# Sliding-window attention under projections: all five queues in one written order, exponentials a round behind, q's rotation in pieces

## The chip, the core and the metric

The kernel runs on one core of one Trainium2 chip. The metric is the time on the device in microseconds (us); of three runs the median is 1564.43 us (1564.02 to 1564.64). The engines are named as in the profile: PE multiplies matrices, PEld loads PE's weights, DVE is the vector engine, ACT the scalar engine, POOL the third elementwise engine, and SP only issues DMAs. Each has a queue of its own.

## What is computed

One decoder layer on 1024 tokens of width 1024: a combined projection, retention and sliding-window attention side by side, a gated merge, and a SwiGLU block. The part that the change touches is the attention, whose core is:

```python
scores = jnp.einsum('bnqhgd,bnkhd->bnhgqk', qb, kb).astype(jnp.float32) * (d ** -0.5)
...
scores = jnp.where(mask[None, :, None, None], scores, -1e30)
sink = sinks.astype(jnp.float32).reshape(1, 1, Hkv, G, 1, 1)
m = jnp.maximum(jnp.max(scores, axis=-1, keepdims=True), sink)
e = jnp.exp(scores - m)
probs = e / (jnp.sum(e, axis=-1, keepdims=True) + jnp.exp(sink - m))
out = jnp.einsum('bnhgqk,bnkhd->bnqhgd', probs.astype(v.dtype), vb)
```

There are 16 query heads of width 64 on 2 key heads, 8 blocks of 128 queries, and each block sees its own 128 keys and the 128 before. Queries and keys are rotated first. Beside it the kernel computes ten of the sixteen 128-column slabs of the two gate projections, `tanh((h @ W + b) / 2)`.

## The kernel before, in words

Every matrix product is made of three: each fp32 operand is split into a high half in a shorter format (a cast on ACT) and a low half (a subtraction on DVE), and high x high, high x low and low x high are added up. `H` holds the normalised input in both halves, transposed.

**Units and rounds.** The 16 heads form four groups g of four heads. A unit u is one group and one block b of queries (u = 8 g + b, 32 units). The loop `for i in range(NU + 2)` makes 34 rounds. Round i transposes the probabilities of unit i - 2 (`u_transpose`, L562), multiplies the scores of unit i (`u_scores`, L530), takes some steps of the fill, and multiplies the values of unit i - 2 (`u_values`, L580). So PE has the fill's products between the transposes and the values that need their result.

**One unit.** Eight products on PE write the scores `s` (negated, for 256 keys; 128 where b is 0). ACT copies the newer half to `sc` (L546), DVE lays the older half over it by a predicated copy (L547) and takes the minimum `nm` with the sink (L549); for b = 0 a custom operation does both (L552). ACT makes four exponentials with their sums (L555), DVE the reciprocal (L558) and the product (L559). PE transposes to `pT` (L567); ACT casts the high half `p` (L569), DVE makes its low half (L570) and a masked copy `q` of both (L575). PE multiplies `p` and `q` with the values to `pv` (L586), ACT copies that to `xy` (L589), and POOL stores it. POOL also writes the sinks into `sc` (L537).

**The fill.** `Fill` runs through a list of products a step (three matmuls) at a time: `QuadQ(1)`, two gates, `QuadQ(2)`, two gates, `QuadQ(3)`, six gates. A `QuadQ` makes the queries of a group, four products of 8 steps (`quad_q`, L478: two token halves by two rotary halves z), a gate two (`gate`, L592). 20 of the 256 steps come ahead of the rounds and 28 behind them; before, the first 16 rounds take 7 steps each and the other 18 some 5.3. `prep` casts an item's weights from a raw slab that SP has loaded (L442 for q, L467 for gates); there are two such slabs, and a load waits until the low half (L452, L473) has read the one before.

**Rotation.** `quad_q` evicts two products to `a` and `b` (ACT, L488), DVE makes six operations with the tables (L497 to L502), ACT and DVE split the result (L503 to L506). The four tiles `a`, `s2`, `s1`, `b` are stored to `q_d` and read back to the layout that the scores want (`send_turned`, L514): four stores and four reads a half, all on SP. `a` and `b` rotate through three buffers, `s1` and `s2` have one each, so the next half must wait for these stores.

**What sets the order.** Each engine works through its queue in order. The order is made when the kernel is built: a scheduler places instructions by priority, and `in_order(...)` pins the written order on the queues that it names. Before, it names PE and SP for the rounds; ACT, DVE and POOL are placed by the scheduler, with chains (`tie`) for the casts and low halves alone. Behind the rounds, DVE's first tiles of the next stage (`vacc`, L731) lie where the attention's tiles lay.

Of the kernel before, what the change touches and what calls it, by code (L numbers as in the profile page):

```python
# [40 lines left out]
def hybrid_block(ctx: ExitStack, tc: tile.TileContext, x, ln1_g, w_in, b_in, ret_norm_g, w_ret_out,  # L41
# [41 lines left out]
    def acc(name):  # L83
        return ps("acc", 3, name)
# [240 lines left out]
    with tc.tile_pool(name="gt", bufs=1, side="right") as gt, tc.tile_pool(name="w1", bufs=1) as w1:  # L325
        atab = w1.tile([P, 2, S], F32, name="atab")
# [6 lines left out]
        vodd = w1.tile([P, NB // 2, P], F32, tag="xy", bufs=2, name="vodd")  # L333
# [144 lines left out]
        def quad_q(g, w):  # L478
            if g % 2 == 0:
                big(B, "B", g // 2, f"q{g}")  # L480
            Bt = B[g // 2]
            jb = (g % 2) * 4
            ab = {}
            for half, z in ((0, 0), (0, 1), (1, 0), (1, 1)):
                pt = acc(f"aq{g}{z}{half}")
                yield from mm_g(pt, w[z], H, half * 512)
                t = r512("rab", 3, f"q{g}{z}{half}")
                nc.scalar.activation(t, pt, AF.Identity, bias=bcol[:, QB + 4 * z + g:QB + 4 * z + g + 1], scale=1.0)  # L488
                ab[z, half] = t
                if z == 0:  # L490
                    yield
                    continue
                c = slice(half * 512, half * 512 + 512)
                a, b = ab[0, half], t
                s1, s2 = (r512(f"st{i}", 1, f"st{i}{g}{half}") for i in (1, 2))
                cos, sin = atab[:, 0, c], atab[:, 1, c]
                nc.vector.tensor_tensor(out=s2, in0=a, in1=cos, op=ALU.mult)  # L497
                nc.vector.tensor_tensor(out=s1, in0=b, in1=sin, op=ALU.mult)
                nc.vector.tensor_tensor(out=s2, in0=s2, in1=s1, op=ALU.subtract)
                nc.vector.tensor_tensor(out=a, in0=a, in1=sin, op=ALU.mult)  # L500
                nc.vector.tensor_tensor(out=b, in0=b, in1=cos, op=ALU.mult)
                nc.vector.tensor_tensor(out=b, in0=b, in1=a, op=ALU.add)  # L502
                nc.scalar.activation(a.bitcast(F32R), s2, AF.Copy)  # L503
                nc.vector.tensor_tensor(out=s2.bitcast(F32R), in0=s2, in1=a, op=ALU.subtract)
                nc.scalar.activation(s1.bitcast(F32R), b, AF.Copy)
                nc.vector.tensor_tensor(out=b.bitcast(F32R), in0=b, in1=s1, op=ALU.subtract)  # L506
                turns.append((q_d[2 * g + half], (a, s1, s2, b), Bt[:, jb:jb + 4, c]))
                if g == 0 and half == 0:
                    send_turned()
                yield  # L510

        turns = []

        def send_turned():  # L514
            for qd, rows, o in turns:
                for r in (0, 2, 1, 3):
                    nc.sync.dma_start(qd[:, r, :], rows[r])
                for r in (0, 2, 1, 3):
                    nc.sync.dma_start(f32(o[r * 32:r * 32 + 32]), qd[:, r, :].rearrange("(j e) c -> e j c", e=32))
            turns.clear()  # L520
# [7 lines left out]
        phs = {}  # L528

        def u_scores(u):  # L530
# [3 lines left out]
            mk = amask[:, 0:P]  # L534
            sc = w1.tile([P, 4, 132], F32, tag="sc", bufs=3, name=f"sc{g}{b}")
            scs[u] = sc
            nc.gpsimd.tensor_copy(sc[:, :, P:P + 1], nsink[:, 4 * g:4 * g + 4].rearrange("p (j o) -> p j o", o=1))  # L537
            nm = tiny.tile([P, 4], F32, tag="nm", name=f"nm{g}{b}")
# [1529 lines left out]
```

## Time and profile before

| what | before |
|---|---|
| median of 3 runs | 1564.43 us |
| the profiled execution | 1560.39 us, its span 1558.6 us |
| mean granted clock of PE | 0.998 |
| PE busy | 1539.6 us, 99% |
| DVE, ACT, POOL busy | 1030.0, 690.5, 404.2 us |
| 78 to 190 us (rounds 0 to 14): PE, DVE, ACT busy of 112 us | 107.58, 81.94, 65.35 us |
| 190 to 305 us (the later rounds): the same of 115 us | 111.22, 87.52, 70.62 us |

The profile is one execution, taken by the hardware profiler; its times are from the span's start. "Idle before" an instruction is time in which its engine did nothing, with what ended that. The chain is the work that ended last, followed back from the last instruction. PE's matmuls overlap, so their durations add up to more than their time.

### The profile page before, as it was taken

How to read it: one execution, taken by the hardware profiler on the slowest of the kernel's cores; microseconds unless marked ns; L12 is line 12 of the kernel's file. 1: busy time of each engine (PE TensorE's matmuls, PEld its weight loads, DVE VectorE, ACT ScalarE, POOL GpSimd, SP SyncE). 2: the span in 40 equal slices, each digit the busy share in tenths (PEclk: the TensorE clock that was granted, in tenths of full speed). 3: DMA queues.
4: the chain of work that ended last, by engine and by line, in shares of the span. 5: the costliest groups of instructions: out<-in, count | busy, mean ns of one | idle time of the engine just before them, and what ended most of it. 6: DMA issues, size and time to landing. Idle time of an engine off the chain costs nothing.

```text
span 1558.6 us, 20393 instructions
## 1 busy us (share of the span) xinstructions
PE 1539.6 (99%) x7311; PEld 1283.1 (82%) x7311; DVE 1030.0 (66%) x1566; ACT 690.5 (44%) x1360; POOL 404.2 (26%) x356
## 2 busy tenths in 40 slices
PE   9999999999999999999999999999999999999998
PEld 8887787788878888888888888888888888888886
DVE  7577787697477683878557788444444444678656
ACT  6355565533334454544223365333333333444445
POOL 2001111100254431000021124655555555100001
PEclk9999999999999999999999999999999999999999
DMA  6663546321777766654555303333333333863233
GB/s 229 194 189 117 162 152 232 134 69 68 202 199 223 216 203 212 228 178 152 181 182 205 146 1 107 105 107 107 108 102 102 101 102 102 305 242 95 89 108 121
DMA packets 159025, 236.86 MB, mean 152 GB/s; under 512 B 10602, under 2 KB 82092, under 8 KB 158668
## 3 DMA queue, kind: packets, MB, share of 16 engines
q1 hardware_dynamic: 156316, 227.04, 45.2%
q0 software_dynamic: 2560, 8.39, 1.4%
q8 instruction: 57, 0.93, 0.3%
q14 instruction: 44, 0.36, 0.1%
q10 hardware_dynamic: 48, 0.13, 0.0%
HBM read 156.62 MB, written 74.19 MB: 148 GB/s over the span
## 4 chain that ended last, share of the span: by engine, by line
PE 88%; DVE 4%; DMA 3%; ACT 2%; issue 1%; SPq 1%; POOL 0%; POOLq 0%; DVEq 0%; ACTq 0%
PE fA L1692 15%; PE fB L1692 8%; PE dA L1994 7%; PE wA L957 7%; PE dxP L1994 6%; PE fC L1692 4%; PE wB L957 3%; PE va L800 3%; PE wo L1526 3%; PE woP L1526 2%; PE vP L800 2%; PE acc_ba L178 2%; PE acc_ba L180 2%; PE acc_ba L179 2%; PE acc_bb L179 2%; PE acc_bb L180 2%
## 5 line engine op out<-in xcount | busy, mean ns | idle before, releaser
L1994 PE MATMUL dA<-dwP,daP 128*128 128x512 f32 x528 | 120.6, 389 | 0.0
L1994 PEld LDWEIGHTS dA<-dwP,daP 128*128 128x128 f32 x528 | 99.1, 188 | 20.7 <-DVE dwP L154 0.2
L1994 PE MATMUL dxP<-dwP,daP 128*128 128x512 f32 x396 | 90.2, 389 | 0.0
L1994 PEld LDWEIGHTS dxP<-dwP,daP 128*128 128x128 f32 x396 | 74.3, 188 | 15.4
L555 ACT ACTIVATE sc<-sc,nm 128x129 f32<-128x129 f32 x128 | 50.1, 394 | 44.3 <-DVE nm L549 32.0
L1767 POOL TENSOR_TENSOR xf<-xf 128x512 f32<-128x512 f32 x40 | 59.9, 1497 | 30.5 <-issue 28.9
L178 PE MATMUL acc_g<-h,wh_g 128*128 128x512 f32 x160 | 62.7, 392 | 0.0
L1698 POOL TENSOR_TENSOR xf<-xf 128x512 f32<-128x512 f32 x33 | 47.3, 1435 | 58.7 <-ACT xf L1700 26.9
L179 PE MATMUL acc_g<-h,wh_g 128*128 128x512 f32 x160 | 62.5, 391 | 0.0
L180 PE MATMUL acc_g<-h,wl_g 128*128 128x512 f32 x160 | 62.3, 389 | 0.0
L537 POOL COPY sc<-nsink 128x4 f32<-128x4 f32 x32 | 10.1, 317 | 189.5 <-PE pT L567 83.1
L1899 POOL TENSOR_TENSOR rs_f<-tot,mhalf 128x1 f32<-128x1 f32 x8 | 4.8, 604 | 205.4 <-DVE tot L1896 205.4
L154 DVE TENSOR_TENSOR dwP<-wd,dwP 128x512 fp32r<-128x512 f32 x77 | 52.8, 686 | 4.8 <-ACT dwP L151 4.8
L151 ACT CAST dwP<-wd 128x512 fp32r<-128x512 f32 x77 | 47.4, 616 | 9.1 <-PE dA L1994 6.9
L178 PE MATMUL acc_bb<-ay,wh_bb 128*128 128x512 f32 x128 | 51.0, 400 | 0.0
L669 POOL TENSOR_TENSOR wr_f<-wr_f 128x512 f32<-128x512 f32 x20 | 30.7, 1533 | 76.0 <-DVE t_18P L154 8.6
L180 PE MATMUL acc_bb<-ay,wl_bb 128*128 128x512 f32 x128 | 50.3, 393 | 0.0
L151 ACT CAST daP<-daP 128x512 fp32r<-128x512 f32 x42 | 26.0, 621 | 54.8 <-PE dxP L1994 26.7
L179 PE MATMUL acc_bb<-ay,wh_bb 128*128 128x512 f32 x128 | 50.2, 392 | 0.0
L178 PE MATMUL aq<-h,wh_aq 128*128 128x512 f32 x128 | 50.1, 392 | 0.0
L179 PE MATMUL aq<-h,wh_aq 128*128 128x512 f32 x128 | 50.0, 391 | 0.0
L178 PE MATMUL acc_ba<-yg,wh_ba 128*128 128x512 f32 x128 | 49.9, 390 | 0.0
(852 smaller groups left out, 4305.2 us busy)
## 6 DMA issues: line engine op xcount, KB each, us to landing
act_d<-xf SPq DMA_DIRECT2D x77, 256.0 KB, 2.1
daP<-act_d SPq DMA_DIRECT2D x21, 512.0 KB, 3.6
q<-q_d SPq DMA_DIRECT2D x32, 256.0 KB, 5.0
xy_d<-xy POOLq DMA_DIRECT2D x32, 256.0 KB, 3.0
wr_daP<-act_d SPq DMA_DIRECT2D x14, 512.0 KB, 6.7
wd<-in_w_ffn_down SPq DMA_DIRECT2D x6, 1024.0 KB
wr_wp<-in_w_in SPq DMA_DIRECT2D x11, 512.0 KB, 3.7
wp<-in_w_in SPq DMA_DIRECT2D x11, 512.0 KB
```

What stands on the lines that cost most here:

```text
L151: nc.scalar.copy(hi, raw)
L154: return nc.vector.tensor_tensor(out=lo, in0=raw, in1=f32(hi), op=ALU.subtract)
L178: nc.tensor.matmul(pt, hi[:, k, :], xh, start=(k == 0), stop=False)
L179: nc.tensor.matmul(pt, hi[:, k, :], xl, start=False, stop=False)
L180: nc.tensor.matmul(pt, lo[:, k, :], xh, start=False, stop=(k == 7))
L555: nc.scalar.activation(sc[:, j, 0:P + 1], sc[:, j, 0:P + 1], AF.Exp, scale=-1.0, bias=nm[:, j:j + 1], accum_out=den[:, j:j + 1])
L800: nc.tensor.matmul(vbanks[pr][tt], x_[:, c], w[:, u, :], start=(fresh and k + z == 0), stop=(k == 3 and z == 2), skip_group_check=not fresh)
L957: nc.tensor.matmul(pt, o[:, w, k, :], v, start=(first and k + z == 0), stop=(k == 3 and z == 2), skip_group_check=not first)
L1526: nc.tensor.matmul(bank, v[:, q + u, k, c], w[y][:, k % 2, :], start=(first and z == 0), stop=(last and z == 2), skip_group_check=not tracked)
L1692: nc.tensor.matmul(pt, o[:, w, k, :], v, start=(first and n == 0), stop=(n == 11), skip_group_check=not first)
L1767: nc.gpsimd.tensor_tensor(out=o, in0=a, in1=b, op=op)
L1994: nc.tensor.matmul(banks[tt], a[:, u, c], w[:, v, :], start=(fresh and f + z == 0), stop=(f == NP - 1 and z == 2), skip_group_check=not fresh)
```

## The change

**One written order.** `in_order` now names all five queues for the rounds. What stood inside `u_scores` becomes four functions: `u_sink` (POOL, a round ahead), `u_scores` (PE alone), `u_min` (copy, predicated copy, minimum) and `u_exp` (exponentials, reciprocal, product), and `u_exp` handles unit i - 1 in round i.

**q by token halves.** `quad_q` goes half by half. Its rotation is cut into three tasks (three products, three products, the split with its stores), and a round takes one task off a list: its ACT part behind `u_min`, its DVE and SP parts behind the fill steps. The eviction of the last product of a group waits in the list too, joined to the first task of its half. A half's read-back is issued in the round after its stores, behind `u_min`. For group 0 all tasks run at once.

**Pacing and the rest.** The first 21 rounds take 140 steps, the other 13 take 68. The four 1 MB loads of `wv` are issued in rounds 20, 22, 24 and 26 instead of all in round 20. `vodd` is the first tile of its pool instead of the seventh. The core of the diff:

```diff
+            for half in range(2):
+                c = slice(half * 512, half * 512 + 512)
+                ab = []
+                for z in range(2):
+                    pt = acc(f"aq{g}{z}{half}")
+                    yield from mm_g(pt, w[z], H, half * 512)
...
+                    if z and half:
+                        tasks.append(([evict], [], []))
+                    else:
+                        evict()
+                    if z:
+                        rotation(g, half, c, ab, Bt[:, jb:jb + 4, c])
+                        if g == 0:
+                            all_tasks()
                     yield
...
+            first = [start, lambda: tt(s2, a, cs, ALU.mult), lambda: tt(s1, b, sn, ALU.mult),
+                     lambda: tt(s2, s2, s1, ALU.subtract)]
+            if tasks and not tasks[-1][1]:
+                tasks[-1][1].extend(first)
+            else:
+                tasks.append(([], first, []))
+            tasks.append(([], [lambda: tt(a, a, sn, ALU.mult), lambda: tt(b, b, cs, ALU.mult),
+                               lambda: tt(b, b, a, ALU.add)], []))
+            tasks.append(([lambda: high(a, s2), lambda: high(s1, b)],
+                          [lambda: low(s2, s2, a), lambda: low(b, b, s1)], [store]))
...
-        early, late = 16 * 7, 96
-        with in_order(nc.tensor.engine, nc.sync.engine):
+        early, late, turn = 140, 68, 21
+        with in_order(nc.tensor.engine, nc.sync.engine, nc.scalar.engine, nc.vector.engine, nc.gpsimd.engine):
+            u_sink(0)
             for i in range(NU + 2):
...
                 if i < NU:
                     u_scores(i)
-                n, i0, m = (early, 0, 16) if i < 16 else (late, 16, NU - 14)
+                if 0 < i <= NU:
+                    u_exp(i - 1)
+                if i < NU:
+                    u_min(i)
+                while reads:
+                    reads.pop(0)()
+                on_act, on_dve, on_sp = task()
+                do(on_act)
+                if i + 1 < NU:
+                    u_sink(i + 1)
+                n, i0, m = (early, 0, turn) if i < turn else (late, turn, NU + 2 - turn)
                 fl.step((i - i0 + 1) * n // m - (i - i0) * n // m)
+                do(on_dve)
+                do(on_sp)
                 if i > 1:
                     u_values(i - 2)
```

Lines of the new kernel that the text names: L492 the eviction, L514 the rotation's products, L530 and L533 the split, L521 and L526 the stores and reads, L581 scores, L590 to L593 copy to minimum, L596 the same for b = 0, L604 exponentials, L607 and L608 reciprocal and product, L616 transposes, L618, L619 and L624 `p`, its low half and `q`, L635 values, L638 the copy to `xy`, L716 the loads of `wv`.

What this does to ACT's queue shows in a round of the second group. Names carry a buffer number; `pT` is read by the cast to `p`, `wh_aq` are high halves of q's weights. Before:

```order
L589 COPY xy_1903<-pv_1898 128x512
L546 COPY sc_1916<-s_1920 128x4x128
L555 ACTIVATE sc_1916,den_1919<-sc_1916,nm_1918 128x129 x4
L451 CAST wh_aq_1889<-wr_aq_1698 128x512
L569 CAST p_1911<-pT_1906 128x512
L597 ACTIVATE tb_1945<-acc_g_0_1873,bhalf 128x512
L589 COPY xy_1969<-pv_1964 128x512
```

After, the same kind of round:

```order
L618 CAST p_1875<-pT_1870 128x512
L604 ACTIVATE sc_1762,den_1764<-sc_1762,nm_1763 128x129 x4
L590 COPY sc_1830<-s_1880 128x4x128
L530 ACTIVATE q_1617<-st_1789 128x512
L530 ACTIVATE st_1788<-q_1760 128x512
L451 CAST wh_aq_1917<-wr_aq_1623 128x512
L451 CAST wh_aq_1917<-wr_aq_1702 128x512
L646 ACTIVATE tb_1932<-acc_g_0_1855,bhalf 128x512
L638 COPY xy_1946<-pv_1941 128x512
```

The cast to `p` moved from behind the exponentials and the weight cast to the head of its round, and the exponentials now read minima of the round before.

SP's queue ahead of the first rounds: `wr_g` are raw slabs of gates, `wr_aq` of q, `q_d` the stores of a turned half, `q_675<-q_d` its read-back. Before:

```order
L519 DMA q_675<-q_d 32x4x512 x4
L467 DMA wr_g_832<-in_w_in 128x8x128
L467 DMA wr_g_834<-in_w_in 128x8x128
L517 DMA q_d<-q_775 128x512
L517 DMA q_d<-st_811 128x512
L517 DMA q_d<-st_810 128x512
L517 DMA q_d<-q_808 128x512
L519 DMA q_675<-q_d 32x4x512 x4
L442 DMA wr_aq_965<-in_w_in 128x4x256
```

After:

```order
L526 DMA q_675<-q_d 32x4x512 x4
L521 DMA q_d<-q_775 128x512
L521 DMA q_d<-st_811 128x512
L521 DMA q_d<-st_810 128x512
L521 DMA q_d<-q_808 128x512
L526 DMA q_675<-q_d 32x4x512 x4
L467 DMA wr_g_840<-in_w_in 128x8x128
L467 DMA wr_g_842<-in_w_in 128x8x128
L442 DMA wr_aq_950<-in_w_in 128x4x256
L442 DMA wr_aq_1013<-in_w_in 128x4x256
```

The loads of the first two gates moved behind the stores and the read-back of the second half of group 0, and the second of group 2's loads moved up: before, it stood behind the read-back of both halves of group 1 (eleven rows further on).

SP's queue where the last group is turned, before:

```order
L467 DMA wr_g_2285<-in_w_in 128x8x128
L517 DMA q_d<-q_2094 128x512
L517 DMA q_d<-st_2204 128x512
L517 DMA q_d<-st_2203 128x512
L517 DMA q_d<-q_2201 128x512
L519 DMA q_1372<-q_d 32x4x512 x4
L655 DMA wv<-in_w_in 128x4x512 x4
```

After:

```order
L467 DMA wr_g_2270<-in_w_in 128x8x128
L716 DMA wv<-in_w_in 128x4x512
L467 DMA wr_g_2399<-in_w_in 128x8x128
L521 DMA q_d<-q_2132 128x512
L521 DMA q_d<-st_2277 128x512
L521 DMA q_d<-st_2276 128x512
L521 DMA q_d<-q_2198 128x512
L526 DMA q_1369<-q_d 32x4x512 x4
L647 DMA tb_d<-tb_2475 128x512
L716 DMA wv<-in_w_in 128x4x512
```

A gate's load and one of `wv` now stand ahead of the stores of the last group's first half, and the other three of `wv` behind.

## Prediction on record

> **What bounds the kernel now.** I read the page's head first, then who waited for whom on PE, then the chain that ended last and the timeline around the attention rounds.
>
> ```profile
> span 1558.6 us, 20393 instructions
> PE 1539.6 (99%) x7311; PEld 1283.1 (82%) x7311; DVE 1030.0 (66%) x1566; ACT 690.5 (44%) x1360; POOL 404.2 (26%) x356
> ```
>
> PE is busy 99% of the span, so only time in which PE doesn't issue can be won, and no edit here takes a matmul away. The waits of PE name the place:
>
> ```profile
> PE pv L586 <- DVE q L575: 5.3, 6, 2.3
> PE pv L586 <- ACT p L569: 1.8, 2, 1.6
> PE pv L586 <- DVE p L570: 1.0, 2, 0.6
> ```
>
> That is 8.1 us, all at the values products of a round, which need the probabilities p (high half from ACT, low half from DVE) and their masked copy q (DVE). The true loss is larger: the view counts idle time from a matmul's modelled end, and matmuls overlap. So I compare PE's pace with the stretch. The chain gives the paces:
>
> ```profile
> 29.95 0.44 PE lnT L240 x4
> 36.60 2.87 PE ak L195 x24
> ...
> 325.13 11.17 PE va L800 x48
> 336.30 10.88 PE vP L800 x48
> ```
>
> 48 products of 512 columns take 10.88 us, 0.2267 each; 256 columns take 2.87 / 24 = 0.12; 128 columns 0.11. Starts of the scores, from PE's timeline:
>
> ```profile
> 78.18 0.33 PE L543 MATMUL s<-kst,q 128*128 128x128 f32 x2
> ...
> 128.74 0.36 PE L543 MATMUL s<-kst,q 128*128 128x256 f32 x1
> 135.82 0.30 PE L543 MATMUL s<-kst,q 128*128 128x128 f32 x1
> ```
>
> From the first scores (78.18) to the first product of the next stage (325.13) are 246.95 us. The code issues there 236 fill steps of three products and 120 values products (828 of 512 columns, 187.7 us), 224 scores of 256 columns (26.8) and 160 products of 128 (17.6): 232.1 us. **PE loses 14.85 us.** A quiet round of 7 steps, 128.74 to 135.82, takes 7.08 against 21 x 0.2267 + 8 x 0.12 + 4 x 0.11 + 4 x 0.2267 = 7.07. I put 34 rounds at 0.04 us of unavoidable loss, 1.4, and **13.5 us** as what a perfect order wins. Two pieces of the chain show how the loss comes about:
>
> ```profile
> 106.32 3.83 DMA q_d<-q
> 110.52 6.92 DMA wr_aq<-in_w_in
> 120.72 0.72 PE pv L586 x2
> ...
> 182.25 1.35 ACT sc L555 x7
> 184.45 0.68 DVE wl_aq L452
> 185.77 1.23 DVE q L575
> 187.04 1.22 PE pv L586 x2
> ```
>
> In the first, SP sat on the read-back of a turned q until its store had landed; the weight load behind it came late, ACT's weight cast waited for it, and p's cast stood behind. In the second, p's cast and q stood behind a round's exponentials and a weight low half.
>
> **The change part by part.** Each queue holds to a written order at run time before and after alike; what changes is the order.
>
> *The order of a round.* I measure from T, the end of a round's transposes. The hand-over in the trace:
>
> ```profile
> 188.26 0.85 PE pT L567 x4
> 189.20 0.58 ACT L569 CAST p<-pT 128x512 fp32r<-128x512 f32 x1 [0.31 <-PE pT L567]
> 189.82 0.69 DVE L570 TENSOR_TENSOR p<-pT,p 128x512 fp32r<-128x512 f32 x1 [2.83 <-ACT p L569]
> 190.54 1.22 DVE L575 SCALAR_TENSOR_TENSOR q<-amask,p 128x1024 fp32r<-128x1024 f32 x1
> 191.68 0.72 DVE L547 COPY_PREDICATED sc<-amask,s 128x512 f32<-128x512 uint32 x1
> ```
>
> With T = 189.11, DVE's p begins at T + 0.7, q ends at T + 2.65, and DVE is free at T + 2.6 (it holds 0.08 less than a duration when the next is ready). The new order puts p first on ACT and p, q first on DVE. PE reaches the values after 0.96 of scores and 15 to 21 fill products (3.4 to 4.8): T + 4.4 at the earliest. So p and q may come 1.7 us late (short rounds) to 3.1 us (long ones) before PE waits. The rest of the round:
>
> ```profile
> L555 ACT ACTIVATE sc<-sc,nm 128x129 f32<-128x129 f32 x128 | 50.1, 394 | 44.3 <-DVE nm L549 32.0 <-DVE nm L552 12.3
> L549 DVE TENSOR_REDUCE nm<-sc 128x4 f32<-128x516 f32 x28 | 19.2, 686 | 1.0
> L473 DVE TENSOR_TENSOR wl_g<-wr_g,wh_g 128x1024 fp32r<-128x1024 f32 x10 | 12.2, 1220 | 0.0
> L558 DVE RECIPROCAL rd<-den 128x4 f32<-128x4 f32 x32 | 5.7, 177 | 36.4 <-ACT sc L555 36.4
> ```
>
> ACT runs p's cast, four exponentials of the round before (4 x 0.39, done by T + 2.2; their minima have long been there) and the copy of the new scores (done by T + 2.75). DVE's reciprocal therefore finds its sums ready when q is done, and predicated copy and minimum follow: p 0.7, q 1.15, reciprocal 0.2, product 0.6, copy 0.8, minimum 0.6, **4.1 us**, free at T + 4.9. The 44.3 us in which ACT waited for minima and the 36.4 in which DVE waited for sums had been between stages of one round; now a round lies between them.
>
> *Rotation in pieces.* A round carries at most 2.0 (three products at 0.6, one waiting on the last) or 1.2 (two low halves) beside 1.15 for a gate's low half or 1.2 for two of q's weights. The budget: early rounds of 6 or 7 steps last 6.4 or 7.08 us (7.08 before in all 16), late ones of 5 steps 5.7 (by the sum above, as before). The heaviest early rounds hold 4.1 + 1.2 + 2.0 = 7.3 against 7.08: hidden. Late, rotation of group 3 meets short rounds: round 21 6.45, rounds 22 and 23 6.1 each, against 5.7: DVE is late by 0.75, 1.15, 1.55. That is under the 1.7, but round 22 adds something: the deferred eviction on ACT and the first product on DVE take buffers that the half before is still storing, and behind them stand the values copy and p of round 23. Stores issued at T + 6.5 of round 21 and landed 5 us later (below) hold them to about T + 6 of round 22, half a microsecond beyond DVE's own lateness. **I take 0.5 us lost there**, between 0 (stores as quick as the quiet ones below) and 1.5.
>
> *q of group 3.* Its first half is turned in rounds 19, 20 and 21 and stored at the end of 21, but the scores of round 24 need it read back. SP's timeline of such pairs, and the landing of a read:
>
> ```profile
> 150.50 0.50 SPq L517 DMA_DIRECT2D q_d<-q  x1
> 155.58 2.84 SPq L519 DMA_DIRECT2D q<-q_d  x4
> 164.25 0.34 SPq L517 DMA_DIRECT2D q_d<-q  x1
> ...
> 166.70 2.75 SPq L519 DMA_DIRECT2D q<-q_d  x4
> ...
> 236.44 0.67 SPq L517 DMA_DIRECT2D q_d<-q  x1
> ...
> 246.08 2.98 SPq L519 DMA_DIRECT2D q<-q_d  x4
> ...
> q<-q_d SPq DMA_DIRECT2D x32, 256.0 KB, 5.0
> ```
>
> SP reaches the first store after the gate load ahead of it, which waits for DVE's gate low half: about T + 6.5 of round 21. A read lands 5.0 us after its issue, so some 4.7 after the end of four issues. From first store to last landing that makes 155.58 + 2.84 - 150.50 + 4.7 = 12.6 us where a weight load stood just ahead, as here; 9.9 from 164.25, which had none; 17.3 from 236.44, behind 4 MB of wv. So q is there at T + 19.1, and the scores of round 24 come at 3 x 5.7 = T + 17.1, plus the 0.5: **1.5 us of waiting**, between 0 and 6.6. Before, this half was stored a round earlier and PE didn't wait for it, so the wait is new; I take the pair from 150.50, since its place in the queue is the same.
>
> [...]
>
> *SP at the start.* The first gate's weights now load behind q's second half and its read-back:
>
> ```profile
> 69.30 1.04 SPq L467 DMA_DIRECT2D wr_g<-in_w_in  x2
> 71.95 1.99 SPq L517 DMA_DIRECT2D q_d<-q  x1
> 79.17 1.82 SPq L519 DMA_DIRECT2D q<-q_d  x4
> ...
> wr_g<-in_w_in SPq DMA_DIRECT2D x8, 512.0 KB, 4.5
> ```
>
> The load moves from 69.30 to somewhere between 77 (stores faster without 1 MB of weights ahead) and 81. It lands at 81.5 to 85.5; ACT's gate cast (1.05) now stands ahead of the first exponentials, and DVE owes low half 1.15, products 2.0, reciprocal and product 0.8 before the first transposes: 86.5 to 90.5. PE gets there at 78.18 + 0.9 + 18 x 0.2267 + 0.96 + 21 x 0.2267 = 88.9. **0.4 us**, between 0 and 1.6. In return the second load of group 2 no longer stands behind a read-back (the chain's first piece).
>
> *At nothing:* sinks on POOL a round ahead (each waits for transposes at the head of its round), wv's four loads two rounds apart (needed from round 25), vodd's other address (the next stage's first tiles still wait for the last rounds, with the 28 fill steps behind them, 28 x 3 x 0.2267 = 19 us, as cover), the fill's pacing (the same 256 steps).
>
> **Sum.** 13.5 - 0.5 - 1.5 - 0.4 = 11.1 won. The profiled execution took 1560.39 (span 1558.6 and 1.8 around it) and would take 1549.3; the median of the runs is 1564.43, 4.0 more, and the same amount off it gives **1553.3**.
>
> **Rivals.**
> *No wait is left.* Stores are quick as from 164.25, nothing above is lost: 1564.4 - 13.5 = 1550.9. Against it: 12.6 and 17.3 us are in the same trace. [...]
> *Transfers decide.* The stores of round 21 land as from 236.44, 9.6 us each (246.08 - 236.44): the scores of round 24 wait 6.6, which takes in the wait of round 23, and two earlier halves, each 1 us past its slack, bring 2: 1564.4 - 13.5 + 8.6 = 1559.5. For it: wv's loads still lie in these rounds; against: one megabyte at a time.
> *DVE paces every round: slower.* If ACT reaches the exponentials x later than T + 0.6, because evictions, a gate's cast and the values copy of the round before hold it, DVE waits in front of the reciprocal in every round, all else stands behind, and p of the next comes late. Its mean room is 6.85 (140 steps in 21 rounds) less 4.1 and some 1.7 of pieces, and late 5.87 (68 in 13) less 4.1 and 1.1; 0.4 more passes until q is done. The loss is 21(x - 1.45) + 13(x - 1.07) = 34x - 44: at x = 1.4, the mean that ACT waited there before (44.3 / 32), it is 3 us; from x = 1.7 it eats the gain, and at 1.8 the time is 1564.4 - 13.5 + 17 = 1568. Against it: ACT is 44% busy over the span.
>
> **How the numbers follow.** My forecast 0.6; no wait 0.15; transfers decide 0.15; DVE paces 0.1. A measurement can tell 0.2%, 3.1 us. The first two lie clear below 1561.3, the third mostly (0.11 of 0.15); the same gets 0.05, slower 0.09, faster 0.86. The bounds of the unknown costs run from 1550.9 to 1564.43 - 13.5 + 1.5 + 6.6 + 1.6 = 1560.6; the range ends there and leaves out the last rival and little else.
>
> **What the profile after would show.** Waits of PE at the values (L635) nearly gone and rounds of 7.1, 6.4 and 5.75 us; one wait at the first scores (L581) of group 3, named with a read-back of q; exponentials (L604) without minima ahead of them. Wrong if PE still waits for q (L624) in rounds without a transfer at their head, if the first wait is elsewhere, or if a stage after 315 us begins to wait.

## The result and the profile after

The changed kernel takes 1553.03 us (median of 6 runs, 1551.76 to 1553.45) beside 1563.57 for the kernel before on the same chip (6 runs, 1559.48 to 1564.64): a ratio of 0.9934, interval 0.9922 to 0.9947. The forecast was 1553.3. The profiled execution took 1553.45, 6.9 less than that of before (1560.39). These two differences, 10.5 and 6.9, are one of the things to explain.

The head of the page after: the same matmuls, and PE as busy as before in a shorter span.

```profile
span 1551.7 us, 20401 instructions
PE 1539.0 (99%) x7311; PEld 1284.6 (83%) x7311; DVE 1026.2 (66%) x1566; ACT 689.4 (44%) x1360; POOL 406.4 (26%) x356
```

PE's waits in the rounds (us in total, times, longest). The 8.1 us at the values have shrunk to 0.5, and there is one new wait, at the scores for the read-back of q:

```profile
PE s L581 <- DMA q<-q_d: 1.5, 1, 1.5
...
PE pv L635 <- DVE q L624: 0.5, 1, 0.5
...
PE pT L616 <- ACT wh_g L472: 0.3, 1, 0.3
```

ACT's exponentials, by line; the last number is the idle time ahead of them, 44.3 us before:

```profile
L604 ACT ACTIVATE sc<-sc,nm 128x129 f32<-128x129 f32 x128 | 50.2, 403 | 0.2
```

DVE waited for their sums 2.6 us in three rounds, after 36.4 in 26.

To see the rounds alone I take the stretch from the first scores to the next stage's first product, as one window: its length, and PE's busy time in it. First before, then after:

```profile
78.18:324.97 246.79, 238.59 (x1214) 198.78 (x1213) 182.73 (x294) 139.68 (x411) 32.07 (x61) 0.99 0.51 164
```

```profile
78.10:318.34 240.24, 237.75 (x1214) 200.35 (x1212) 185.17 (x294) 137.70 (x410) 31.84 (x61) 0.99 0.53 170
```

The stretch lost 6.55 us. PE's idle time in it fell from 8.20 to 2.49, but PE is "busy" 237.75 us with work that the issue rates price at 232.1. So PE still loses 8.1 us, of which only 2.5 are waits. Its timeline shows where most of the rest is:

```profile
236.60 0.73 PE L635 MATMUL pv<-q,vdf 128*128 128x512 f32 x2 [0.47 <-DVE q L624]
237.51 0.63 PE L616 MATMUL pT<-ident,sc 128*128 128x128 f32 x4 [0.18 <-DVE sc L608]
239.67 1.94 PE L581 MATMUL s<-kst,q 128*128 128x128 f32 x8 [1.53 <-DMA q<-q_d]
...
241.94 0.63 PE L179 MATMUL acc_g<-h,wh_g 128*128 128x512 f32 x1
242.37 0.63 PE L180 MATMUL acc_g<-h,wl_g 128*128 128x512 f32 x1
...
246.33 0.40 PE L178 MATMUL acc_g<-h,wh_g 128*128 128x512 f32 x1
246.56 0.40 PE L179 MATMUL acc_g<-h,wh_g 128*128 128x512 f32 x1
...
248.30 1.20 PE L581 MATMUL s<-kst,q 128*128 128x256 f32 x8
```

After the wait of 1.53 the products of 512 columns start 0.43 us apart (241.94 to 242.37), and 0.23 again from 246. The trace's record of the granted clock says 0.5 from 239.12 for 6.83 us. In the kernel before it says 0.5 from 187.03 for 3.41 us, right behind the waits of 184 to 187.

My theory: the new order removed the losses as forecast, and the waits left are those forecast; but a wait costs more than its length, since it can halve PE's clock behind it. Rivals: the waits left are transfers that vary from one execution to the next; or not all parts of the change do something, so that, say, the exponentials' place or the written order on ACT and DVE is idle.

### The profile page after: what moved, and what is told of

It is laid out like the page before. It is cut to its first block, busy times and chain, and to the rows that moved or that the text cites. A ratio compares the mean times of both kernels' runs of the same rounds, so it can differ in the third digit from the quotient of the medians.

```text
span 1551.7 us, 20401 instructions
## 1 busy us (share of the span) xinstructions
PE 1539.0 (99%) x7311; PEld 1284.6 (83%) x7311; DVE 1026.2 (66%) x1566; ACT 689.4 (44%) x1360; POOL 406.4 (26%) x356
## 4 chain that ended last, share of the span: by engine, by line
PE 92%; DMA 3%; DVE 2%; issue 1%; ACT 1%; SPq 0%; POOL 0%; POOLq 0%; DVEq 0%; ACTq 0%
PE fA L1753 15%; PE fB L1753 8%; PE dA L2055 7%; PE wA L1018 6%; PE dxP L2055 6%; PE fC L1753 4%; PE wB L1018 3%; PE va L861 3%; PE wo L1587 3%; PE acc_g L178 2%; PE acc_g L179 2%; PE acc_g L180 2%; PE woP L1587 2%; PE vP L861 2%; PE acc_ba L179 2%; PE acc_ba L180 2%
## 5 line engine op out<-in xcount | busy, mean ns | idle before, releaser
L1828 POOL TENSOR_TENSOR xf<-xf 128x512 f32<-128x512 f32 x40 | 63.2, 1580 | 30.5 <-issue 28.9
L639 POOL DMA_DIRECT2D xy_d<-xy x32 | 23.1, 721 | 179.3 <-ACT xy L638 90.2
L1759 POOL TENSOR_TENSOR xf<-xf 128x512 f32<-128x512 f32 x33 | 47.3, 1434 | 58.8 <-ACT xf L1761 26.9
L604 ACT ACTIVATE sc<-sc,nm 128x129 f32<-128x129 f32 x128 | 50.2, 403 | 0.2
```

The source lines that it names most:

```text
L604: nc.scalar.activation(sc[:, j, 0:P + 1], sc[:, j, 0:P + 1], AF.Exp, scale=-1.0, bias=nm[:, j:j + 1], accum_out=den[:, j:j + 1])
L1828: nc.gpsimd.tensor_tensor(out=o, in0=a, in1=b, op=op)
```

## The experiments

All in one table: the stretch of the rounds and PE's busy time in it from the profiles, and the times against the kernel before. e1 and e12 are single executions; e2 to e4, e5 to e8 and e9 to e11 shared a chip each, with 1561.52, 1562.38 and 1562.49 for the kernel before.

| kernel | stretch | PE busy | median | ratio to before |
|---|---|---|---|---|
| before | 246.79 | 238.59 | 1563.57 | 1 |
| e1 before again | 246.46 | 238.39 | 1562.25 | |
| e12 before, third time | 248.18 | 240.10 | 1562.77 | |
| after | 240.24 | 237.75 | 1553.03 | 0.9934 [0.9922, 0.9947] |
| e5 after again | 239.79 | 237.80 | 1551.22 | 0.9932 [0.9920, 0.9945] |
| e2 fill first | 238.99 | 236.64 | 1551.12 | 0.9928 [0.9916, 0.9941] |
| e3 exponentials in the same round | 271.71 | 248.11 | 1586.64 | 1.0153 [1.0137, 1.0169] |
| e4 three queues free | 242.62 | 237.64 | 1555.30 | 0.9960 [0.9947, 0.9972] |
| e6 ten products more | 237.80 | 236.91 | 1551.89 | 0.9935 [0.9922, 0.9947] |
| e7 loads behind stores | 235.10 | 234.54 | 1548.24 | 0.9911 [0.9898, 0.9925] |
| e8 other pacing | 235.46 | 233.96 | 1548.71 | 0.9912 [0.9899, 0.9926] |
| e9 e7 and e8 | 233.57 | 233.57 | 1546.95 | 0.9899 [0.9882, 0.9917] |
| e10 wv at once | 241.27 | 238.19 | 1554.66 | 0.9952 [0.9937, 0.9967] |
| e11 rotation in one go | 251.53 | 241.39 | 1564.71 | 1.0016 [1.0007, 1.0025] |

The span outside the stretch runs from 1310.3 to 1314.9 us in these profiles, whatever the kernel (the code there is the same): for example, e1 waited 1.16 us at 534 us for a low half of the next stages' weights (w6P), where the first execution of before had no such wait. That is noise that the medians carry and the stretch does not.

### e1: the kernel before again

No edit.

> The kernel before, unchanged, profiled a second time. If PE's waits in the attention rounds are fixed by the written order, they stand at the same places with the same sizes (within 0.3 us), and only the stretch in which the granted clock falls to 0.5 (3.4 us from 187.0 in the first profile) may come, go or grow; the time then moves with that stretch, by up to the 5 us between the fastest and the slowest run seen. If the waits themselves move by over 1 us from one execution to the next, the 5 us are the transfers' and not the clock's.

The stretch came out at 246.46 for 246.79, with the same stalls at the same places: rounds 5, 14 and 22 lost 3.5, 3.1 and 2.55 us (3.6, 3.2 and 2.55 in the first), and the clock fell to 0.5 at 186.87, for 3.41 us again. So the waits belong to the order. The 1.9 us by which this execution's span is longer lie outside the stretch.

### e3: the exponentials in the round of their minima

```diff
-                if 0 < i <= NU:
-                    u_exp(i - 1)
                 if i < NU:
                     u_min(i)
+                    u_exp(i)
```

> The changed kernel, but each round's exponentials stand in the round of their minima, as in the kernel before; all else as changed (five queues in a written order, p and q first, rotation in groups). Theory one, the round between minima and exponentials is what takes ACT's and DVE's waits for each other away: DVE now holds p 0.7, q 1.15, copy 0.8, minimum 0.6, then waits 1.6 for four exponentials, then 0.8, 5.7 a round, with 1.7 of pieces early and 1.1 late, 7.4 against 6.85 and 6.8 against 5.87; 21 x 0.55 + 13 x 0.93 = some 24 us slower than the changed kernel, and so some 13 slower than the kernel before. Theory two, p and q at the head of the round are what matters and the exponentials' place does not: within 3 us of the changed kernel.

It is slower than the kernel before, by 25 us where I had 13; than the changed kernel by 31.5 in the stretch, more than the 24 that I had. DVE's waits and, by line, ACT's exponentials:

```profile
DVE rd L607 <- ACT sc L604: 52.1, 32, 1.7
```

```profile
L604 ACT ACTIVATE sc<-sc,nm 128x129 f32<-128x129 f32 x128 | 50.1, 393 | 112.5 <-DVE nm L593 100.3 <-DVE nm L596 12.2
```

Each of the 32 reciprocals waits 1.6 us, the four exponentials' length, as theory one had it, and PE then waits at the values (11.5 us in 18 rounds for q, 7.8 in 10 for p). With a fixed order on DVE these waits can't be filled with other work. So theory two falls: a written order with the exponentials in place is worse than the order before, in which the scheduler places DVE's work, and the round between minima and exponentials is what makes the new order pay. The sum fell short by 7.5. The clock was halved three times here (from 122.39, 200.89 and 252.09), but for 3.41 us each, 10.2 in all beside 6.83 after, so it accounts for at most 1.7 of that; where the rest went is open. PE's idle time alone rose by 21.1 us (23.6 for 2.49).

### e4: ACT, DVE and POOL placed by the scheduler

```diff
-        with in_order(nc.tensor.engine, nc.sync.engine, nc.scalar.engine, nc.vector.engine, nc.gpsimd.engine):
+        with in_order(nc.tensor.engine, nc.sync.engine):
```

> The changed kernel's program, but only PE and SP hold to the written order; ACT, DVE and POOL are placed by the scheduler in the attention rounds, as in the kernel before. Theory one, the written order on ACT and DVE carries the gain: p and q stand behind rotation pieces and low halves again in some rounds, PE waits there, and 3 to 10 us of the gain are lost. Theory two, what carries it is the code's own order (exponentials a round behind, rotation in groups, which the scheduler can follow without being told): within 2 us of the changed kernel.

The stretch is 2.4 us longer than after, the median 1555.30 beside 1561.52 before: the code's new order keeps about two thirds of the gain in the stretch (4.2 of 6.55), and pinning it on the three queues adds the rest. That is a balance of three parts: rounds 1 and 2 are 3.7 us longer than after, rounds 22 to 24 are 5.4 shorter, and what comes behind them is 4.1 longer. The first loss has one cause. ACT's timeline (the READ_ACCUMULATOR rows left out) and PE's behind it:

```profile
85.24 0.57 ACT L590 COPY sc<-s 128x512 f32<-128x512 f32 x1
87.61 0.41 ACT L604 ACTIVATE sc<-sc,nm 128x129 f32<-128x129 f32 x1 [1.81 <-DVE nm L593]
...
89.17 1.98 ACT L472 CAST wh_g<-wr_g 128x1024 fp32r<-128x1024 f32 x2
```

```profile
90.25 0.50 PE L178 MATMUL acc_g<-h,wh_g 128*128 128x512 f32 x1 [1.75 <-ACT wh_g L472]
...
91.51 0.50 PE L180 MATMUL acc_g<-h,wl_g 128*128 128x512 f32 x1 [0.52 <-DVE wl_g L473]
```

The scheduler put the first gate's cast behind exponentials that wait for a minimum; in the written order it stands ahead (84.13). PE waits 2.27 us, and the clock is halved from 92.26 for 3.41. In rounds 22 to 24 the free order is the better one: the first store of q goes 5.4 us behind the scores of round 21 (228.46 for 223.01), 7.7 after; the wait for q is 0.60, and the clock stays full (the run's mean is 0.998, that of after 0.997). Behind them PE waits 1.95 us in five places, 0.97 of it for `q` of a unit. My "3 to 10" was a little high, and the dearest place is a weight, not p and q.

### e2: work ahead of the scores that wait

```diff
+                if i == 3 * NB:
+                    fl.step(steps)
+                    steps = 0
                 if i < NU:
                     u_scores(i)
```

> The changed kernel, but in round 24 the fill's five steps (15 products, 3.4 us) come ahead of the scores, so that PE has work while q of group 3 lands. Theory one, a wait of 1.5 us and behind it a stretch of 6.8 us at a granted clock of 0.5 that costs another 2.4: both go, the profile shows no granted clock under 0.9 near 240 us, and the kernel takes about 4 us less than the changed kernel (some 1549). Theory two, the halved clock comes from the shorter waits at the values in rounds 22 and 23 and not from this one: only 1.5 goes, some 1551.9. Theory three, q is later than the wait showed because other work released it: PE waits at the scores again, a round's fill later, and nothing is won.

Theory one holds for the wait and the clock of round 24: both losses are gone, while the shorter waits ahead of it (0.41 and 0.17) stayed, which speaks against theory two. But the stretch shrank by 1.25 us only, for new waits came in the next round:

```profile
PE pT L616 <- DVE sc L608: 1.4, 2, 1.3
...
PE s L581 <- DVE nm L596: 0.4, 1, 0.4
```

The five steps took a gate's end with them: its eviction and the next cast now stand ahead of the exponentials on ACT (238.58 and 239.17, 1.7 us), its low half ahead of the reciprocal on DVE (1.2). So the product came 1.3 us late, and the clock fell again, from 245.49 for 3.41. An edit that should move PE's work alone moved that of three queues.

### e5: the changed kernel again

No edit.

> The changed kernel, unchanged, on the chip of the three kernels that follow. The granted clock's halves so far begin on one grid of 3.413 us in each execution (before: 187.03 and 1555.78; changed: 239.12 and 1549.84), and each follows a stretch of the grid in which PE idled 1.6 us or more. If that is so, the wait of 1.5 us at the scores of round 24 comes again with the same size, and whether the clock is halved after it depends on where the grid cuts it: one stretch takes it whole and the clock falls, or two share it and it doesn't, and then the kernel is about 2 us quicker in the rounds 23 and 24. If the halving follows the wait itself, it is there again for 6.8 us.

The wait is 1.20 us this time, round 24 lasts 8.74 us (8.63 in the first), and the clock is 0.5 from 239.14 for 6.83 again. This execution and the first have their grid at almost the same phase, so it could not tell the two readings apart. Its other runs say something: two of them, 1549.54 and 1551.22 us, have a mean granted clock of 0.999, which leaves room for at most 4.7 us at half speed in the whole run; so there the clock wasn't halved for 6.83 us behind the wait, though how long PE waited is not known. The kernel before shows the same in traces in e12, below.

### e6: ten products more

Ten products of 512 columns, read by nobody, ahead of the scores of round 24:

```diff
+                if i == 3 * NB:
+                    pt = ps("t", 2, "busy")
+                    for _ in range(10):
+                        nc.tensor.matmul(pt, vdf[:, 0, 0, :], H[0][:, 0, 0:512], start=True, stop=True)
```

> The changed kernel with ten products of 512 columns more (2.27 us of work that nobody reads) ahead of the scores of round 24, where PE waited 1.5 us for the read-back of q. Theory one, idle PE costs a halved clock on top of the wait: PE has no wait there, the granted clock stays at 1.0, and the kernel is 2.27 - 1.5 - 2.3 = some 1.5 us quicker than the changed kernel although PE has more to do. Theory two, the halved clock costs nothing of its own (the matmuls were slow for another reason, such as the loads of weights beside them): 2.27 - 1.5 = 0.8 us slower, and the matmuls behind the scores take 0.43 us each as before.

```profile
237.93 2.55 PE L697 MATMUL busy<-h,vdf 128*128 128x512 f32 x10
240.32 1.00 PE L581 MATMUL s<-kst,q 128*128 128x128 f32 x8
...
241.45 0.40 PE L179 MATMUL acc_g<-h,wh_g 128*128 128x512 f32 x1
...
245.94 1.19 PE L581 MATMUL s<-kst,q 128*128 128x256 f32 x8
```

The scores take 1.00 us for 1.94, a product behind them 0.40 for 0.63, and the granted clock is full (1.00 from 235.54 to 245.78). From the scores of round 24 to those of round 25 the same instructions take 245.94 - 240.32 = 5.62 us, where the changed kernel takes 248.30 - 239.67 = 8.63: **the halved clock cost 3.0 us**, twice the wait that set it off. With 2.27 us more to do the stretch is 2.0 to 2.4 us shorter, for 1.5 expected. The medians don't show it (1551.89 beside 1551.22); the span outside the stretch was 1313.4 in this profile, near its upper end.

### e7: a round's weight loads behind its stores

```diff
-            load_ahead()
+            if not held_loads[0]:
+                load_ahead()
...
                 do(on_sp)
+                load_ahead()
```

> The changed kernel, with a round's weight loads issued behind its stores of a turned half instead of ahead. Theory one, the read-back of group 3's first half is late because its stores stand on SP behind a gate's load and share the engines with it: from first store to landing it takes about 10 us instead of 12.6, the wait of 1.5 at the scores of round 24 goes, and the halved clock with it: some 4 us quicker than the changed kernel. Theory two, the stores are late because DVE's last pieces are (they end with the gate's low half ahead of them): the stores move by no more than 0.4 us, the wait stays above 1, and the time stays.

SP's timeline, after and e7:

```profile
226.49 0.37 SPq L467 DMA_DIRECT2D wr_g<-in_w_in  x1
226.91 0.72 SPq L521 DMA_DIRECT2D q_d<-q  x1
...
228.72 1.17 SPq L521 DMA_DIRECT2D q_d<-q  x1
231.74 2.29 SPq L526 DMA_DIRECT2D q<-q_d  x4
```

```profile
222.31 0.34 SPq L521 DMA_DIRECT2D q_d<-q  x1
226.71 0.81 SPq L521 DMA_DIRECT2D q_d<-st  x2
227.62 0.40 SPq L521 DMA_DIRECT2D q_d<-q  x1
228.11 0.41 SPq L467 DMA_DIRECT2D wr_g<-in_w_in  x1
228.57 3.22 SPq L526 DMA_DIRECT2D q<-q_d  x4
```

SP no longer waits for a free slab ahead of the stores, so the first store goes 4.6 us earlier, and the last 1.1, with no half megabyte loading beside them; the first read is issued 3.2 earlier and the last 2.2 (at 231.49 for 233.73). The wait fell to 0.55. Since buffers came free earlier too (DVE's first product of the next half, which waited 0.90 us for a store after, waits for none), PE no longer waited for the masked copy `q` in round 23. The clock stayed full (1.00 over the stretch), and the median is 1548.24, 3 us under that of e5. Theory one holds for the wait and the time, but not by its own measure: from the first store to the end of the wait it is 15.0 us, where I expected about 10, since the second store now waits for DVE's low half, which ends at 226.68. From the second store it is 10.6. So DVE's lateness, theory two's cause, now sets when the stores go.

### e8: longer rounds beside the rotation

```diff
-        early, late, turn = 140, 68, 21
+        pace = [0, 140, 166, 208]
+        turns = [0, 21, 25, NU + 2]
```

> The changed kernel with another pacing of the fill: 26 steps in rounds 21 to 24 (21 before) and 42 in the last nine rounds (47 before); the rounds in which group 3 is rotated are then as long as the early ones. Theory one, the losses left in rounds 22 to 24 come from short rounds beside rotation and its stores: the 4 steps more in rounds 21 to 23 are 2.7 us, more than the 1.5 that q was late, and DVE is no longer late for p and q; the waits there go (2.2 us), the halved clock with them (2.3), and the kernel takes some 1549. Theory two, the transfers stretch with the rounds (they begin later by as much): the wait stays at 1 to 1.5. A third outcome: the last nine rounds, now 4 or 5 steps, become too short for DVE (4.1 and a low half of 1.2), and PE waits for p or q there.

The waits at p and q went, and PE came to the scores of round 24 at 239.2 instead of 238.1: of the 2.7 us more of fill some 1.6 only made up for losses that were gone. The reads came 0.7 later (to 234.75), so a wait of 1.36 stayed (the view names an engine that had long been done; it ended 5.8 us behind the end of the last read's issue, after and in e7 5.6 and 5.5, so I take it for the read). So theory two is right for the wait, and yet the time fell to 1548.71: the clock stayed full (1.00 over the stretch), and PE idled 1.0 us less in the stretch. This is the window of the grid with the wait in it:

```profile
238.65:242.07 3.42, 2.06 (x16) 1.77 (x15) 3.38 (x5) 2.62 (x10) 0.91 (x2) 1.00 0.99 371
```

PE is idle 1.36 of 3.42 us, 40%. The last nine rounds held.

### e9: e7 and e8 together

> The two edits of the last call together: a round's weight loads behind its stores, and 26 steps of fill in rounds 21 to 24. Alone, the first left 0.6 us of waiting at the scores of round 24 (its reads were issued 3.2 us earlier), the second 1.4 (PE came 1.1 later). If the wait is what is left of the read-back's time, the two take 3.2 and 1.1 off 1.5, so nothing is left of it, PE waits in none of the rounds 21 to 25, the clock stays full there, and the rounds 1 to 31 lose some 1.4 us in all over their nominal time (2.8 and 3.2 with one edit): 1 to 1.5 us quicker than either, some 1547. If the reads wait for the engines and not for their issue, some 0.5 stays.

```profile
78.20:311.77 233.57, 233.57 (x1213) 198.16 (x1212) 184.85 (x294) 137.30 (x410) 30.79 (x61) 1.00 0.55 175
```

PE is busy in every moment of the stretch, which is 1.47 us over the price of its products, and the median is 1546.95 (4 runs, 1545.30 to 1548.36), 4.3 under that of e5 on another chip, by ratios 0.9899 beside 0.9932. This is the version to keep: it beats both kernels.

### e10: wv at once

```diff
-                if 2 * NB + 4 <= i < 3 * NB + 4 and i % 2 == 0:
...
+                if i == 2 * NB + 4:
+                    wv = act.tile([P, 16, 512], F32, tag="B", name="wv")
+                    for q in range(4):
```

> The changed kernel with the four loads of wv (4 MB) issued together in round 20, as in the kernel before, instead of two rounds apart. Theory one, transfers decide: the stores of group 3's first half, issued some 13 us later, still stand behind the 4 MB, take up to 9.6 us as in the kernel before, and the scores of round 24 wait 3 to 6.6 us instead of 1.5, with a halved clock behind: 2 to 5 us slower than the changed kernel. Theory two, 4 MB at the 305 to 360 GB/s seen near 240 us have passed in 11 to 13 us, the stores find the engines free, and the reads no longer share them with wv: the wait is 1.5 or less.

Between the theories. The reads are issued 1.7 us later than after (233.44 for 231.74) and the scores wait 1.09; ahead of that the buffers come free later, and PE waits 0.84 for p and 0.76 for q:

```profile
235.81 0.50 PE L635 MATMUL pv<-p,vev 128*128 128x512 f32 x1 [0.30 <-ACT p L618]
236.85 0.49 PE L635 MATMUL pv<-p,vev 128*128 128x512 f32 x1 [0.54 <-DVE p L619]
238.11 0.74 PE L635 MATMUL pv<-q,vdf 128*128 128x512 f32 x2 [0.76 <-DVE q L624]
...
240.73 0.66 PE L581 MATMUL s<-kst,q 128*128 128x128 f32 x2 [1.09 <-DMA q<-q_d]
```

The wait is under 1.5 only since PE itself came 1.5 us later, at 239.64 for 238.14; from the first store to the first read's issue it is 6.7 us for 4.8, so the stores landed later, against theory two's free engines. The stretch is 1.0 and 1.5 us longer than in the two profiles of after. The loads two rounds apart are worth about that; transfers matter, but don't decide.

### e11: a half's rotation in one round

```diff
-                on_act, on_dve, on_sp = task()
-                do(on_act)
+                parts = [task() for _ in range(len(tasks))] or [task()]
+                do(parts[0][0])
...
+                for part in parts[1:]:
+                    for steps in part:
+                        do(steps)
```

> The changed kernel with a half's rotation in one round instead of three (same operations; the stores are issued in that round, two earlier). Theory one, the pieces are what keeps p and q in time: DVE holds 4.1 + 3.6 + 1.2, and a gate's low half in some rounds, and waits about 1.2 for ACT's two casts, 10 to 11 us against 7.08 early and 5.7 late; less the 1.7 to 3.1 that p and q may be late, each of the four early halves of groups 1 and 2 loses about 1 us and each of group 3 about 3, 10 us in all, while the wait for q (1.5) and the halved clock behind it (2.3) go: some 6 us slower than the changed kernel, with waits for p and q in each of these rounds. Theory two, the slack of a round is enough for a whole half: 3 to 4 us quicker.

The stretch is 11.5 us longer than after, twice what I expected, and all of the gain is gone. The wait for q did go; in its place:

```profile
PE pT L616 <- DVE sc L608: 4.5, 3, 4.2
PE pv L635 <- ACT p L618: 2.3, 2, 1.2
PE pv L635 <- DVE q L624: 1.9, 3, 0.8
```

What I had missed is ACT: its two casts of the split wait for DVE's six products, and behind them on ACT stand the exponentials. In round 1 ACT sat 5.16 us ahead of the casts, and PE 4.17 ahead of the transposes. The pieces keep three queues in time, not one.

### e12: the kernel before, a third time

> The kernel before, unchanged, profiled a third time. By the medians the change won about 10 us, by the two pairs of profiles 6.6 between the first scores and the next stage's first product (246.8 and 246.5 before, 240.2 and 239.8 after), and the rest of the program varies from 1310 to 1315 whatever the kernel. If the kernel before loses a varying time in the attention rounds (its stalls of 115 to 121 and 234 to 241 us fill 32 to 48% of a stretch of the 3.413 us grid each, near where the clock was halved), a third execution may show a second halved stretch and 248 to 250 us there; if not, 246.5 comes a third time, and the 3 us between the two counts lie outside the attention rounds, where the two kernels are the same.

248.18 us, with the same stalls, and the clock halved at another of them: 0.5 from 119.42 for 6.83 us, and full behind the stall at 189, where it was halved in the first two profiles. Three windows of the grid from the first profile of before (us, then PE's busy time, near the end the clock granted):

```profile
115.35:118.77 3.42, 1.79 (x9) 1.18 (x7) 1.54 (x5) 2.96 (x11) 0.00 (x0) 1.00 0.85 320
118.77:122.18 3.41, 2.30 (x12) 1.55 (x13) 1.86 (x3) 1.08 (x3) 0.00 (x0) 1.00 0.21 79
183.62:187.03 3.41, 1.82 (x6) 0.74 (x4) 3.30 (x5) 1.55 (x3) 0.00 (x0) 1.00 0.21 77
```

And the first stall in the third profile:

```profile
116.00:119.42 3.42, 1.40 (x6) 0.63 (x4) 2.28 (x5) 2.56 (x8) 0.00 (x0) 1.00 0.54 210
119.42:122.83 3.41, 2.88 (x9) 2.08 (x10) 1.11 (x1) 0.68 (x2) 0.00 (x1) 0.50 0.21 77
```

The grid lies 0.65 us later against the program. In the first its line cuts the stall into 1.63 and 1.11 us idle, and the clock stays; in the third 2.02 lie in one window, and the next two run at half. So the same stall can cost a halved clock in one execution and not in the next, and the place where the grid cuts it fits. Idle time in a window doesn't settle it alone, though: 1.63 us (115.35) left the clock full, and 1.59 (183.62), in the same execution, were followed by a halved one.

## Why the prediction was right, and what it missed

**What can be won: right.** The prediction said that 13.5 of 14.85 us were to be had and 1.4 would stay. e9 has 13.2 of them, and 1.47 stays.

**The order of a round: right.** p and q first and a round between minima and exponentials took the 44.3 us of ACT and the 36.4 of DVE to 0.2 and 2.6, and rounds 2 to 21 run at their issue rates. e3 shows that it is this round between that does it.

**Rotation in pieces, 0.5: right in place, too small in size.** As forecast, a transfer holds the first product of the next half (0.90 us, at 232.67), and `q` of round 23 comes late. The idle time is 0.47 for `q` and 0.18 at the transposes behind it. But the sum counted lengths: a round of 5 steps takes 5.73 us (rounds 21 and 27), round 22 took 6.11, and round 23, without its wait of 1.53, 7.11. That is 1.76 us, more than the 1.5 that was its bound. The prediction gave p and q 1.7 us of room and didn't ask when the next transposes need DVE's product, which is as late:

```profile
229.64 0.69 DVE L608 TENSOR_TENSOR sc<-sc,rd 128x512 f32<-128x512 f32 x1
```

```profile
230.48 0.63 PE L616 MATMUL pT<-ident,sc 128*128 128x128 f32 x4
```

The product ends at 230.33, and the transposes start 0.64 us behind the start of the products ahead of them (229.84), where rounds 21 and 22 have 0.47; the view counts no idle time there. e11 shows what whole halves would have cost.

**q of group 3, 1.5: right,** 1.53 and, the second time, 1.20. From the first store to the scores are 239.67 - 226.91 = 12.8 us, for the 12.6 taken from the pair with a load ahead of it. Against the end of round 21's transposes (219.44) the first store came 1.0 us later than I had it, and PE at the scores 1.1 later; that these cancelled is luck. The chain shows the two transfers:

```profile
228.72 4.99 DMA q_d<-q
...
233.73 5.80 DMA q<-q_d
```

**The start, 0.4: right:** 0.30 of idle time at the first transposes, and round 1 is 0.44 longer than in e9.

**The sum: wrong, by a term that wasn't in it and one that was too small.** It left 2.4 us of loss. Idle time left is 2.49, which looks like it. But the stretch after is 6.67 us longer than that of e9, and by the rounds this is 0.44 at the start, 1.76 for the rotation, 1.53 for q and 3.0 for the halved clock of round 24 (e6). The sum took a wait to cost its length and had nothing for the clock behind it. So the profiled execution came to 1553.45, where the sum gave 1549.3: 4.1 too little, most of it the clock and 1.3 the rotation.

**From the profile to the median: right by luck in part.** I took the gain off the median, 4.0 above the profiled execution, as if that difference would stay. But it was the profile of before that lay low: 42 executions of that kernel now have a median of 1562.46 (1559.48 to 1565.98), 11 of the changed one 1552.99 (1549.54 to 1554.04). That is 9.5 us by all executions; the profiles give 7.1 for the stretch (mean of three before, 247.1, of two after, 240.0). A part of the spread is shown: the clock is halved behind one stall or another, at the longer of them 1.4 to 1.7 us dearer in the stretch (e12), and the span outside the stretch varies by 4.6. The clock seems to make up some 1.4 of the 2.4 between, by an estimate from each run's mean granted clock (what it lacks of 1, times the span): the kernel before lost 4.6 us to it in the mean of 36 runs, the changed kernel 3.4 in 11; the profiled executions lost 4.3 and 4.5. So the two profiles of after are ones with a long halved stretch. The rest is not settled. That the forecast of 1553.3 met 1553.03 is luck: a sum 4 us too good, and a difference between profiles and medians that went the other way.

**What the profile would show.** Rounds last 7.10, 6.41 and 5.73 us as forecast, the new wait is at the first scores of group 3, and the span outside the stretch is the same (1311.5 for 1311.8).

**The rivals.** No wait left: the changed kernel isn't that, but e9 is, and it won 13.2 us of the rival's 13.5 in the stretch. Its median, 1546.95 for 1550.9, lies 15.5 under that of the kernel before on its chip; the 2.3 more are again the difference between profiles and medians. Transfers decide: no; even with wv at once it is 1 us (e10). DVE paces every round: not here, but that is what e3 is, when the reciprocals wait.

## What to carry to other kernels

Price a wait of PE not by its length alone: look at the granted clock behind it (here a wait of 1.53 us was followed by 6.83 us at half the clock, which cost 3.0 more), and put other work into a stall of 1.5 us if it can't be removed; here ten unread products ahead of it were worth 2.0 to 2.4 us more than they cost, in the stretch of the rounds if not in the medians. When queues hold to a written order, put a round between two engines that answer each other (without it, in e3, the stretch was 31.5 us longer), and check on every queue what else moves with the step that you move. And place loads behind the stores whose read-back somebody waits for (in e7 the wait fell from 1.53 to 0.55 us). Last, measure what an engine loses by the lengths of its rounds: the idle time that the view counts was 0.65 us of the 1.76 that the rotation cost.

## What the runs showed of the hardware

The shortest halved stretch in the first profile of before lasts 3.413 us (from 187.03), and the times at which the granted clock fell inside one execution lie whole steps of this length apart: there 187.03 and 1555.78, 401 steps; in the first profile of after 239.12 and 1549.84, 384 steps; in e3 122.39 and 200.89, 23 steps. In the rounds it fell behind steps in which PE was idle 1.59 us (before, from 183.62), 1.63 (after, from 235.71), 1.62 (e2, from 242.08) and 2.02 (e12, from 116.00). It did not fall behind 1.63 (before, from 115.35), behind 1.36 (e8, from 238.65), or behind any other step in the rounds of the first profiles of before and after, none of which had more than 1.13. So the idle time of a step does not tell alone whether the clock falls: the same 1.63 us came before a halved clock in one profile and a full one in the other. In the profile of after, the step ahead of the fall and the first of the two behind it:

```profile
235.71:239.12 3.41, 1.78 (x8) 0.72 (x6) 3.27 (x6) 1.81 (x4) 0.00 (x0) 1.00 0.79 247
239.12:242.54 3.42, 2.87 (x11) 2.71 (x12) 3.35 (x6) 2.53 (x10) 1.53 (x2) 0.50 0.97 375
```

The 1.63 us of idle time in the first are gaps of 0.47 and 0.18 us and the first 0.98 of the 1.53.
